# Up-projection by a Strassen-like scheme: weight sums made by adding DMAs, products accumulated in PSUM

## The chip, the cores and the metric

The kernel runs on one core of a Trainium2 chip. A core has a matrix engine (TensorE, PE in the profile; its weight loads are PEld), a vector engine (VectorE, DVE), a scalar engine (ScalarE, ACT), a general engine (GpSimd, POOL) and a sync engine (SP) that here only issues transfers (DMAs). Engines run side by side, each through its own instructions in order, and wait for each other through semaphores. SBUF is the working memory of 128 partitions; PSUM takes the products of TensorE in eight banks of 128x512 float32. The metric is device time in microseconds (us), the median of several runs.

## The reference

One layer of a decoder on 1024 tokens of width 1024: a mixer (pooling, a recurrence and a gate) with its output projection, then a squared-ReLU MLP, then a gated embedding, then a final norm. What matters here is the MLP:

```python
z = rms_norm(h, norm_mlp_g[l])                                    # [1024, 1024]
h = h + jnp.square(jax.nn.relu(z @ w_up[l])) @ w_down[l]          # w_up [1024, 4096]
```

Everything is float32.

## The kernel before

**Tiles and products.** Each float32 operand is split into a high part, rounded to the format that TensorE multiplies, and a low remainder. A product is hi·hi + hi·lo + lo·hi, three matmuls. `split` (L181) makes the parts: ScalarE copies the high part (L184), VectorE subtracts it (L185).

**The up-projection** (`up_first`, `up_pair`; tiles `ps_P_u`) computes 256 of the 4096 columns at a time, a pair of 128-column blocks, so 16 pairs (`NPAIR`). A pair is a 2x2 block product with both the 1024 rows of the weight and the 1024 tokens cut in two. A scheme of the Strassen-Winograd kind makes it with seven block products P1 to P7 instead of eight. Each product has four row tiles times three matmuls of 128x128 by 128x512, that is 12 matmuls (`product`, L815, through `mm`, L357). Four of the seven need sums of weight blocks, and the four results are sums of products. Sums of activation blocks are made once, at the end of the output projection (L790 to L796), and stay in the `a` and `y` tiles as split operands: P6, P7, P4 and P5 read `a`, and P1, P2 and P3 read `y`.

**Weights.** `up_step` brings them in four steps a pair. `load_up` (L240) loads the pair's blocks A11, A12, A21 and A22 with two 512 KB DMAs on SP's queue. VectorE makes the sums in place (`dv`, L226, rows of L227), and two products at a time are split into a high and a low tile (`split_weights`). For the first pair GpSimd makes three of the sums (`gp`, L229) in the tile `rstd` (called `R` in the code) and in the raw tile. There are two high and two low weight tiles of two products each. The list `todo` holds all weight steps of the kernel in order, and `weights()` (L353) starts the next step before it hands out the oldest, so weights are one step ahead of the product that uses them.

**Results.** Each product has a PSUM bank of its own. ScalarE copies some out (`copy`, L864) and VectorE adds the others to them (`add_got` and `add_both`, through `add`, L823). `finish_up` (L842) multiplies by the norm and clips at zero (L845, VectorE), squares (L847, ScalarE), makes four sums for the down-projection (L227) and stores seven blocks by four DMAs (L858, L859). It runs for a pair after the second product of the next one. The result tiles `cc` alternate between two pairs.

**Around it.** Before it stands the output projection (`ps_o`), whose last matmul ends at 225.5 us. In it the second norm collects its squares (`norm.add`, L408) in `T[4]`, with `T[5]` as its scratch; the norm itself is used in pair 1 (four matmuls `n_ps`, L438 and L439). Behind it stands the down-projection (`ps_P_d`), whose operands take the place of the `y` tiles (`open_down`) and of one half of the `a` tiles (`prepare`), as the last pair leaves them.

**Order.** The order on each engine is made ahead of time by a planner that follows the order of the program as its priority and issues an instruction once, by its own estimates, what it needs is ready. On the chip each engine then keeps that order.

Of the kernel before, what the change touches and what calls it, by code (L numbers as in the profile page):

```python
# [13 lines left out]
P = 128  # L14
# [48 lines left out]
def block_kernel(  # L63
# [152 lines left out]
    def split_weights(name, *srcs):  # L216

        hi, lo = weight_tiles(name)
        n = 0
        for src in srcs:  # L220
            w = src.shape[-1]
            split(src, hi[:, n : n + w], lo[:, n : n + w])
            n += w
        return [(hi[:, hs], lo[:, hs]) for hs in HALVES]

# [3 lines left out]
    def gp(op, to, x, y):  # L229
        return nc.gpsimd.tensor_tensor(to, x, y, op).ins  # L230

    up_raw, up_spare, up_lower, up_fourth = {}, [], {}, []

    def load_up(m):  # L240
        if m >= NPAIR:
            return
        up_raw[m] = [raw_tile(f"wu{m}_{i}") for i in range(2)] if m % 2 == 0 else up_spare
        for i, hs in enumerate((slice(0, S), slice(S, 2 * S))):
            nc.sync.dma_start(up_raw[m][i], w_up[m][:, hs])

    def up_blocks(m):
        a, b = up_raw[m]
        return a, b, a[:, FIRST], a[:, SECOND], b[:, FIRST], b[:, SECOND]

    def up_step(m, step):
        name = f"wu{m}_{step}"
        if m == 0:
            if step == 0:
                load_up(0)
            a, b, a11, a12, a21, a22 = up_blocks(0)
            s1, s2 = (R[:, hs] for hs in HALVES)
            if step == 0:
                gp(ALU.add, s1, a21, a22)
                gp(ALU.subtract, s2, s1, a11)  # L260
                gp(ALU.subtract, a21, a11, a21)
                return split_weights(name, s2, a21)
            if step == 1:
                w = split_weights(name, a22, s1)
                load_up(1)
                return w
            if step == 2:
                w = split_weights(name, a11, a12)
                up_lower[0, 3] = lowest[0]
                dv(ALU.subtract, a12, a12, s2)  # L270
                return w
            return split_weights(name, a12)
        a, b, a11, a12, a21, a22 = up_blocks(m)
        s1 = T[5][:, HALVES[m % 2]]
        if step == 0:
            w = split_weights(name, a)
            with tc.issue_after(up_lower[m - 1, 3]):
                dv(ALU.add, s1, a21, a22)
            with tc.issue_after(lowest[0]):
                dv(ALU.subtract, a11, s1, a11)  # L280
                up_fourth[:] = [dv(ALU.subtract, a12, a12, a11)]
            return w
        if step == 1:
            w = split_weights(name, a)

            dv(ALU.subtract, a21, a22, a11)
            load_up(m + 1)
            return w
        w = split_weights(name, b if step == 2 else s1)
        up_lower[m, step] = lowest[0]  # L290
        return w

# [48 lines left out]
    todo += [(up_step, m, step) for m in range(NPAIR) for step in range(4)]  # L341
# [424 lines left out]
    for o in range(NT):  # L766
        nc.sync.dma_start(H[o], xT[o * P : (o + 1) * P, :])
        if o == 0:

            out_w = {0: weights(), 1: asked.pop(0)}  # L770
            for i in range(2):
                out_ps[i] = psum(f"ps_o{i}")
                out_parts(i, out_w[i], out_ps[i], range(NT - 2))
        elif o == 1:
            ask()
        else:
            out_w[o], out_ps[o] = weights(), psum(f"ps_o{o}")
# [12 lines left out]
        if o % 2 == 1:  # L790
            z11, z12, z21, z22 = (T[i][:, hs] for i in range(2) for hs in HALVES)
            t2, t3, t4, t1 = (T[i][:, hs] for i in (2, 3) for hs in HALVES)
            for to, x, y in ((t1, z12, z11), (t2, z22, t1), (t3, z22, z12), (t4, z21, t2)):
                nc.vector.tensor_tensor(to, x, y, ALU.subtract)
            split(T[2], *A[o // 2])
            split(T[3], *A[4 + o // 2])  # L796
# [37 lines left out]
    def twice(x):  # L834
        return x.unsqueeze(1).broadcast_to([P, 2, x.shape[-1]])

    def up_sums(m):
        cc = t_all[:, 2 * (m % 2) : 2 * (m % 2) + 2]
        c11, c12, c21, c22 = (cc[:, i, hs] for i in range(2) for hs in HALVES)
        return cc, c11, c12, c21, c22, T[4 if m else 5][:, HALVES[m % 2]]  # L840
# [40 lines left out]
    done = []  # L881

    def up_first():
        cc, c11, c12, c21, c22, s = up_sums(0)
        ps = {}
        ws = {}
        for kinds in (("P6", "P7"), ("P4", "P5")):
            for kind, w in zip(kinds, weights()):
                ws[kind] = w
                ps[kind] = mlp_bank(f"ps_{kind}_u0")  # L890
                product(ps[kind], w, lambda t, kind=kind: up_operand(kind, t), range(3))
        for kind in ("P6", "P7", "P4", "P5"):
            product(ps[kind], ws[kind], lambda t, kind=kind: up_operand(kind, t), range(3, 4))
        with tc.issue_after(up_lower[0, 3]):
            up_second(NT - 1)
            norm.add(H[NT - 1])
            copy(s, ps["P5"])
            norm.casts()
        ws["P1"], ws["P2"] = weights()
        ws["P3"], _ = weights()  # L900
        for kind in ("P1", "P2"):
            ps[kind] = mlp_bank(f"ps_{kind}_u0")
            product(ps[kind], ws[kind], lambda t, kind=kind: up_operand(kind, t))
        product(ps["P5"], ws["P3"], lambda t: up_operand("P3", t), more=True)
        copy(c11, ps["P1"])
        add_got(c12, ps["P6"], c11)
        add_got(c22, ps["P7"], c12)
        add_got(c11, ps["P2"])
        add_got(c21, ps["P4"], c22)
        add(c22, s)  # L910
        add_got(c12, ps["P5"])
        done.append((0, cc))

    def up_pair(m):
        cc, c11, c12, c21, c22, s = up_sums(m)

        def of(kind, w):
            ps = mlp_bank(f"ps_{kind}_u{m}")
            product(ps, w, lambda t: up_operand(kind, t))
            return ps  # L920

        wa, wb = weights()
        if m == NPAIR - 1:
            preload_down()
        copy(s, of("P1", wa))
        add_got(c11, of("P2", wb), s)
        if m > 1:
            store_up = finish_up(*done.pop())
            if m < NPAIR - 1:
                store_up()  # L930
        else:
            norm.rstd(R, norm.sums(cast=True))
            leave("hl")
        wa, wb = weights()
        copy(c12, of("P3", wb))
        add_got(s, of("P6", wa))
        wa, wb = weights()
        if m == NPAIR - 1:
            with tc.issue_after(open_down()):
                store_up()  # L940
        add_got(c22, of("P7", wa), s)
        if m == NPAIR - 1:
            ask()
            prepare(0, 0)
        add_got(c21, of("P4", wb), c22)
        if m == 1:
            with tc.issue_after(up_lower[1, 2]):
                finish_up(*done.pop())()
        wa, _ = weights()
        p5 = of("P5", wa)  # L950
        if m == NPAIR - 1:
            for tp in range(1, NQ):
                prepare(0, tp)

        with tc.issue_after(up_fourth[0]) if m < NPAIR - 1 else ExitStack():
            add_both(cc[:, :, SECOND], p5)
        add(c12, s)
        done.append((m, cc))


# [6 lines left out]
    def open_down():  # L967
# [9 lines left out]
        for q in range(2, NQ):  # L977
            load_w(0, 0, q)
# [30 lines left out]
    def down(n):  # L1009
# [3 lines left out]
        def operand(t):  # L1013
            return half(A[4 * (n % 2) + t // 2], t % 2)

        for q in range(NQ):
# [13 lines left out]
            if n == q == 0:  # L1030
# [4 lines left out]
                finish_up(*done.pop())()  # L1035
# [54 lines left out]
    for m in range(1, NPAIR):  # L1090
        up_pair(m)
    norm2 = Norm("n2", T[0], T[1:2])
# [382 lines left out]
```

## Time and profile before

| | before |
|---|---|
| median of three runs | 919.4 us (919.05 to 919.93) |
| span of the profiled execution | 917.9 us |
| that execution's own time | not listed apart; the runs lie 1.5 us above its span |
| TensorE busy | 910.4 us, 99% of the span, 4227 matmuls |
| VectorE busy | 762.9 us, 83% |
| ScalarE busy | 443.5 us, 48% |
| GpSimd busy | 27.0 us, 3% |
| DMA, hardware queue | 128.38 MB, 42.0% of 16 engines |
| up-projection | 225.49 to 516.46 us |

A row of a group names the line, the engine, the operation, output and input tiles by the program's names, their shapes and the count; then the busy time, the mean in ns of one, and the idle time of the engine just before them with what ended it. A row of the chain has a start, a length and what filled it. L367 is the helper that issues nearly all matmuls; the tile tells the stage. `SPq` is SP's DMA queue.

### The profile page before, as it was taken

To read this page: it belongs to the slowest core of one execution; us is meant where nothing else is said; L and a number is where in the kernel's file an instruction comes from. 1 tells how busy PE (TensorE), PEld (TensorE's weight loads), DVE (VectorE), ACT (ScalarE), POOL (GpSimd) and SP (SyncE) were. 2 spreads that over 40 slices of the span, in tenths; PEclk is the share of its full clock that TensorE was granted. 3 is DMA by queue.
4 is the path that set the end of the run, shared out by engine and by line. 5 is a ranking of instruction groups with operands and counts; after the bars stand their busy time and mean duration, and the time that the engine had idled before them with its cause. 6 is when DMAs were issued, how large, how long until landed. Compare 5 with 4: busy or idle time off the path is not lost.

```text
span 917.9 us, 10985 instructions
## 1 busy us (share of the span) xinstructions
PE 910.4 (99%) x4227; PEld 792.5 (86%) x4227; DVE 762.9 (83%) x892; ACT 443.5 (48%) x517; POOL 27.0 (3%) x38
## 2 busy tenths in 40 slices
PE   9999999999999999999999999999999999999997
PEld 7888888888888888888888888888888888888886
DVE  7898984669998888888888989899877579799676
ACT  6568992447543343334333654344343346656223
POOL 3400000002000000000000000000000000000001
PEclk9999999999999999999999999999999999999999
DMA  8311143211255345435543998466633341032353
GB/s 270 101 51 32 38 169 107 69 46 62 77 164 192 127 154 195 156 126 172 198 135 135 320 370 279 132 197 208 200 112 125 114 161 47 1 115 70 93 183 126
DMA packets 49636, 129.07 MB, mean 141 GB/s; under 512 B 4400, under 2 KB 9392, under 8 KB 49584
## 3 DMA queue, kind: packets, MB, share of 16 engines
q1 hardware_dynamic: 49584, 128.38, 42.0%
q8 instruction: 33, 0.54, 0.2%
q14 instruction: 19, 0.16, 0.1%
HBM read 92.71 MB, written 35.65 MB: 140 GB/s over the span
## 4 chain that ended last, share of the span: by engine, by line
PE 98%; issue 1%; DVE 0%; DVEq 0%; ACT 0%; POOLq 0%; POOL 0%
PE ps_P_u L367 32%; PE ps_P_d L367 32%; PE ps_i L367 9%; PE ps_o L367 9%; PE ps_e L367 8%; PE ps_l L367 3%; PE ps_e L1223 2%; PE ps_l L574 1%; PE ps_j L367 1%; PE ps_g L643 1%; PE ps_p L367 1%; PE ps_l_second L367 1%; PE ps_l L524 0%; PE ps_j L1247 0%; PE ps_e L1247 0%
## 5 line engine op out<-in xcount | busy, mean ns | idle before, releaser
L367 PE MATMUL ps_P_d<-a,wd_P_hi 128*128 128x512 f32 x880 | 261.7, 379 | 0.0
L367 PEld LDWEIGHTS ps_P_d<-a,wd_P_hi 128*128 128x128 f32 x880 | 166.3, 189 | 23.6
L367 PE MATMUL ps_P_d<-a,wd_P_lo 128*128 128x512 f32 x440 | 166.8, 379 | 0.0
L367 PE MATMUL ps_P_u<-a,wu_hi 128*128 128x512 f32 x512 | 152.3, 379 | 0.0
L367 PE MATMUL ps_P_u<-y,wu_hi 128*128 128x512 f32 x384 | 114.2, 379 | 0.0
L367 PEld LDWEIGHTS ps_P_u<-a,wu_hi 128*128 128x128 f32 x512 | 96.8, 189 | 13.8
L367 PE MATMUL ps_P_u<-a,wu_lo 128*128 128x512 f32 x256 | 97.0, 379 | 0.0
L367 PEld LDWEIGHTS ps_P_d<-a,wd_P_lo 128*128 128x128 f32 x440 | 83.2, 189 | 12.0
L367 PEld LDWEIGHTS ps_P_u<-y,wu_hi 128*128 128x128 f32 x384 | 72.6, 189 | 10.2
L823 DVE TENSOR_TENSOR t_h<-t_h,ps_P_u 128x512 f32<-128x512 f32 (+1 forms) x80 | 62.5, 781 | 20.2 <-PE ps_P_u L367 20.2
L367 PE MATMUL ps_P_u<-y,wu_lo 128*128 128x512 f32 x192 | 72.8, 379 | 0.0
L823 DVE TENSOR_TENSOR t_h<-t_h,ps_P_d 128x512 f32<-128x512 f32 (+1 forms) x56 | 42.5, 759 | 33.5 <-PE ps_P_d L367 33.5
L185 DVE TENSOR_TENSOR a<-wd,a 128x1024 fp32r<-128x1024 f32 x56 | 67.2, 1219 | 1.1 <-ACT a L184 0.8
L367 PE MATMUL ps_i<-a,wi_hi 128*128 128x512 f32 x256 | 66.1, 381 | 0.0
L367 PE MATMUL ps_o<-y,wo_hi 128*128 128x512 f32 x256 | 65.7, 379 | 0.0
L184 ACT ACTIVATE a<-wd 128x1024 fp32r<-128x1024 f32 x56 | 58.2, 1051 | 14.3 <-PE ps_P_d L367 7.0
L184 ACT ACTIVATE wu_hi<-wu 128x1024 fp32r<-128x1024 f32 x24 | 25.4, 1057 | 69.7 <-PE ps_P_u L367 48.4
L184 ACT ACTIVATE wu_hi<-wu_raw 128x1024 fp32r<-128x1024 f32 (+1 forms) x26 | 25.2, 975 | 66.6 <-PE ps_P_u L367 39.5
L367 PEld LDWEIGHTS ps_i<-a,wi_hi 128*128 128x128 f32 x256 | 48.1, 189 | 8.0 <-issue 0.7
L367 PEld LDWEIGHTS ps_o<-y,wo_hi 128*128 128x128 f32 x256 | 48.4, 189 | 6.9
L367 PEld LDWEIGHTS ps_P_u<-a,wu_lo 128*128 128x128 f32 x256 | 48.4, 189 | 6.8
L184 ACT ACTIVATE wd_P_hi<-wd 128x1024 fp32r<-128x1024 f32 x24 | 25.3, 1055 | 53.2 <-PE ps_P_d L367 51.4
(258 smaller groups left out, 1497.1 us busy)
## 6 DMA issues: line engine op xcount, KB each, us to landing
wd<-act SPq DMA_DIRECT2D x56, 512.0 KB, 5.4
act<-t_h SPq DMA_DIRECT2D x32, 512.0 KB, 4.7
wu_raw<-in_w_up SPq DMA_DIRECT2D x16, 512.0 KB, 3.9
wu<-in_w_up SPq DMA_DIRECT2D x16, 512.0 KB, 4.0
act<-wu SPq DMA_DIRECT2D x16, 512.0 KB, 5.0
wd<-in_w_down SPq DMA_DIRECT2D x16, 512.0 KB, 5.6
t_h<-in_xT SPq DMA_DIRECT2D x14, 512.0 KB, 4.6
wg_raw<-in_w_gate SPq DMA_DIRECT2D x10, 512.0 KB, 3.3
```

The lines of the kernel that those rows point to most:

```text
L184: first = pin(nc.scalar.activation(hi, src, AF.Copy))
L185: lowest[:] = [pin((eng or nc.vector).tensor_tensor(lo, src, f32(hi), ALU.subtract)).ins]
L367: ins = nc.tensor.matmul(ps, w, turns(z[:, hs]), start=first and z is zhi and w is whi, stop=last and w is wlo, skip_group_check=more,)
L574: nc.tensor.matmul(ps, kblk(w, o), turns(z[:, hs]), start=k == n == 0, stop=False)
L643: nc.tensor.matmul(x, w[r, o * P : (o + 1) * P], turns(z[r, at : at + HALF]), start=n == 0, stop=n == 2)
L823: (eng or nc.vector).tensor_tensor(to, to if y is None else y, x, ALU.add)
L1223: nc.tensor.matmul(pg, z, turns(quad[x == 1][:, k]), start=n == 0, stop=n == 3 * NT - 1, skip_group_check=True)
```

## The change

Only the up-projection and its edges change. The seven products remain, 12 matmuls each.

- The signs of the scheme change so that the weight of P3 is the sum of all four blocks, P6's is A21 + A22 + A11, P5's A21 + A22 and P7's A21 + A11 (P1 takes A11, P2 A12, P4 A22).
- The weight sums are made by DMAs that add to what lies in their destination (`grow`, issued by GpSimd). A tile is loaded with A21 twice, one adding DMA of both halves makes P5's and P7's weights, and once P5's is split a second one makes P6's, then a third P3's in the same place. Each adding DMA waits until both parts of the split before it are made. Pair 0's tile is made in `R` during the output projection (`seed_up`). The last pair's P3 has a tile of its own.
- The weights are split product by product (`up_weight`), into one tile that holds the high and the low half; there are four of these tiles. `up_first` begins with one more `ask()`, so weights are two products ahead. A22 has a tile of its own (half of `T[5]`), and loads for a pair start up to two pairs ahead.
- In the middle pairs products are accumulated on each other in PSUM: ScalarE copies P1 out negated into the bank of P6, and P6, P7 and (in the next pair) P4 are accumulated onto it; P2 is accumulated onto P1's bank and P3 onto P5's. ScalarE copies the sums out in between; VectorE takes two differences a pair (`take`).
- The order of the products becomes P1, P5, P4 of the pair before, P6, P2, P3, P7. The last pair has an order of its own (`up_last`): P1, P5, P2, P3, P4 of the pair before, P4, P6, P7, and the down-projection's first operands take the other half of the `a` tiles.
- The host lays the weight out in the order A22, A11, A12, A21.

The core of the diff:

```diff
-    def split_weights(name, *srcs):
...
-    def gp(op, to, x, y):
-        return nc.gpsimd.tensor_tensor(to, x, y, op).ins
...
+    up_raw, up_lower, up_spare, up_place = {}, {}, [], itertools.cycle(("whi", "wlo"))
+    A22, A11, A12, A21 = (slice(n * HALF, (n + 1) * HALF) for n in range(4))
+
+    def twice(x):
+        return x.unsqueeze(1).broadcast_to([P, 2, x.shape[-1]])
+
+    def grow(to, src):
+        nc.gpsimd.dma_start(to, src, accum_op=ALU.add)
+
+    def seed_up():
+
+        halves = R.rearrange("p (y s) -> p y s", y=2)
+        nc.sync.dma_start(halves, twice(w_up[0][:, A21]))
+        for x in range(2):
+            grow(R[:, HALVES[x]], w_up[0][:, A22])
+        grow(R[:, SECOND], w_up[0][:, A11])
 
     def load_up(m):
...
+        a, c = [raw_tile(f"wu{m}_{i}") for i in range(2)] if m % 2 == 0 else up_spare
+        up_raw[m] = a, c, T[5][:, HALVES[m % 2]], c[:, FIRST] if m else R[:, SECOND]
+        w = w_up[m]
+        if m:
+            nc.sync.dma_start(c.rearrange("p (y s) -> p y s", y=2), twice(w[:, A21]))
+            grow(c, w[:, : 2 * HALF])
+        else:
+            nc.sync.dma_start(c[:, SECOND], w[:, A21])
+            grow(c[:, SECOND], w[:, A11])
+        nc.sync.dma_start(a, w[:, A11.start : A12.stop])
+        nc.sync.dma_start(up_raw[m][2], w[:, A22])
+        if m == NPAIR - 1:
+            nc.sync.dma_start(T[4][:, FIRST], w[:, A21])
+            for x in (A22, A11, A12):
+                grow(T[4][:, FIRST], w[:, x])
...
+    def up_weight(m, kind):
...
+        w = wp.tile([P, S], F32R, tag=next(up_place), name=f"wu{m}_{kind}")
+        hi, lo = (w[:, hs] for hs in HALVES)
+        split(src, hi, lo)
+        up_lower[m, kind] = lowest[0]
+        if kind == "P5" and not first:
+            grow(chain, w_up[m][:, A11])
+        elif kind == "P6" and not last:
+            grow(chain, w_up[m][:, A12])
+        elif kind == ("P4", "P3")[first] and m < NPAIR - 2:
+            load_up(m + 2)
+        elif first and kind == "P7":
+            load_up(1)
+        return hi, lo
...
             out_w = {0: weights(), 1: asked.pop(0)}
+            seed_up()
...
+    def up_open(m):
+
+        cc, c11, c12, c21, c22 = up_sums(m)
+        a, d = bank(f"ps_a_u{m}"), bank(f"ps_d_u{m}")
+        up_product(m, "P1", a)
+        if m < NPAIR - 1:
+            chains[m] = banks(f"ps_b_u{m}")[:, :HALF]
+            nc.scalar.activation(chains[m], a, AF.Copy, scale=-1.0)
+        else:
+            copy(c12, a)
+        up_product(m, "P5", d)
+        copy(c22, d)
+        return a, d
+
+    def up_fourth(m):
+        cc, c11, c12, c21, c22 = up_sums(m)
+        ps = chains.pop(m)
+        up_product(m, "P4", ps, more=True)
+        copy(c21, ps)
+        return finish_up(m, cc)
 
     def up_pair(m):
...
+        a, d = up_open(m)
+        b = chains[m]
         if m > 1:
+            up_fourth(m - 1)()
         else:
             norm.rstd(R, norm.sums(cast=True))
             leave("hl")
...
+        up_product(m, "P6", b, more=True)
+        copy(c12, b)
+        up_product(m, "P2", a, more=True)
+        copy(c11, a)
+        up_product(m, "P3", d, more=True)
+        take(c12, d, c12)
         if m == 1:
...
+            finish_up(0, up_sums(0)[0])()
+        up_product(m, "P7", b, more=True)
+        take(c22, b, c22)
...
-                split(X[tp], *A[4 * (n % 2) + tp])
+                split(X[tp], *A[4 * ((n + 1) % 2) + tp])
...
-    wu = np.asarray(w_up)[0].reshape(NT // 2, 2, P, NPAIR, 2, P).transpose(3, 2, 4, 1, 0, 5)
+    wu = np.asarray(w_up)[0].reshape(NT // 2, 2, P, NPAIR, 2, P).transpose(3, 4, 1, 2, 0, 5)
+    wu = np.stack([wu[:, i, j] for i, j in ((1, 1), (0, 0), (0, 1), (1, 0))], axis=2)
```

More of the change, by code (lines that the diff above doesn't have):

```diff
@@ L1 @@
+import itertools
 from contextlib import ExitStack
@@ L240, in load_up @@
-    def load_up(m):
[L241 to L291, printed above, removed]
@@ L905, in up_first @@
+        up_product(0, "P3", ps["P5"], more=True)
         copy(c11, ps["P1"])
-        add_got(c12, ps["P6"], c11)
-        add_got(c22, ps["P7"], c12)
+        take(c12, ps["P6"], c11)
+        add_got(c21, ps["P7"], c12)
         add_got(c11, ps["P2"])
[L909 to L912, printed above, removed]
-    def up_pair(m):
[L915 to L926, printed above, removed]
+        dv(ALU.subtract, c22, c21, c22)
@@ L976, in open_down @@
             last = load_x(0, tp)
-        for q in range(2, NQ):
-            load_w(0, 0, q)
+        load_w(0, 0, 2)
         for q in range(2):
@@ L1089, in block_kernel @@
     up_first()
-    for m in range(1, NPAIR):
+    for m in range(1, NPAIR - 1):
         up_pair(m)
+    up_last()
     norm2 = Norm("n2", T[0], T[1:2])
```

131 lines of the change are left out of this document (70 added, 61 removed).

## The prediction

> **What bounds the kernel now.** I read the page first, then the chain of waits in order of time, then the up stage by windows, then its instructions by shape. The first two fences are the page's head and rows of the chain (start in us, length in us, what).
>
> ```profile
> span 917.9 us, 10985 instructions
> PE 910.4 (99%) x4227; PEld 792.5 (86%) x4227; DVE 762.9 (83%) x892; ACT 443.5 (48%) x517; POOL 27.0 (3%) x38
> ```
>
> ```profile
> 225.49 23.34 PE ps_P_u L367 x108
> 248.83 0.22 PE n_ps L438
> ...
> 249.47 0.22 PE n_ps L439
> 249.69 266.77 PE ps_P_u L367 x1236
> 516.46 290.09 PE ps_P_d L367 x1344
> ...
> 899.79 5.19 PE ps_e L1223 x24
> 904.98 0.02 issue
> ```
>
> The up-projection runs from 225.49 to 516.46, 290.97 us, with 108 + 4 + 1236 = 1348 matmuls: 0.2158 us each. The down-projection next to it, which the change leaves its matmuls, needs 290.09 / 1344 = 0.2158. The pieces of the chain join end to end and all are TensorE's, so the stage holds no stall that a lighter VectorE could give back. The windows say the same (busy time and count per engine, granted clock, DMA share, GB/s).
>
> ```profile
> core 0: us, PE busy (x) PEld busy (x) DVE busy (x) ACT busy (x) POOL busy (x), PEclk, DMA share, GB/s
> 225.00:516.00 291.00, 291.00 (x1350) 254.63 (x1349) 259.07 (x305) 121.11 (x145) 0.00 (x0) 1.00 0.47 157
> 516.00:806.00 290.00, 290.00 (x1346) 253.80 (x1345) 238.76 (x240) 132.73 (x142) 0.00 (x0) 1.00 0.50 169
> ```
>
> VectorE is 89% busy in the stage (259.07 of 291) and TensorE 100% at a granted clock of 1.00. VectorE is nearly full, but it is nobody's wait.
>
> **The change part by part.** The matmuls first: seven products of 12 matmuls for each of 16 pairs, before and after; no size, clock or operand width changes. Cost 0. One product is 12 x 0.2158 = 2.59 us, a pair 18.13.
>
> VectorE and ScalarE, by shape inside the stage (count, busy us and mean ns of one, idle before):
>
> ```profile
> L823 DVE TENSOR_TENSOR t_h<-t_h,ps_P_u 128x512 f32<-128x512 f32 x65 | 44.3, 681 | 20.2 <-PE ps_P_u L367 20.2
> L845 DVE SCALAR_TENSOR_TENSOR t_h<-t_h,rstd 128x2048 f32<-128x2048 f32 x15 | 34.3, 2284 | 0.0
> L185 DVE TENSOR_TENSOR wu_lo<-wu,wu_hi 128x1024 fp32r<-128x1024 f32 x24 | 29.3, 1221 | 1.8 <-ACT wu_hi L184 1.3
> L184 ACT ACTIVATE wu_hi<-wu 128x1024 fp32r<-128x1024 f32 x24 | 25.4, 1057 | 69.7 <-PE ps_P_u L367 48.4 <-DVE wu L227 19.8 <-PE n_ps L439 1.5
> L864 ACT ACTIVATE t_h<-ps_P_u 128x512 f32<-128x512 f32 x32 | 18.7, 587 | 6.1 <-PE ps_P_u L367 5.9
> L823 DVE TENSOR_TENSOR t_h<-t_h,ps_P_u 128x1024 f32<-128x1024 f32 x14 | 17.0, 1214 | 0.0
> L227 DVE TENSOR_TENSOR wu<-t_h,wu 128x512 f32<-128x512 f32 x8 | 5.5, 691 | 0.2
> L185 DVE TENSOR_TENSOR wu_lo<-t_h,wu_hi 128x512 fp32r<-128x512 f32 x15 | 10.3, 684 | 0.0
> L184 ACT ACTIVATE wu_hi<-t_h 128x512 fp32r<-128x512 f32 x15 | 9.5, 630 | 12.8 <-PE ps_P_u L367 12.8
> ```
>
> Removed from VectorE: the four weight sums of pairs 1 to 15, 60 x 0.69 = 41 us, and most sums of products: 65 + 14 reads of PSUM fall to 5 (pair 0), 28 (two in each of pairs 1 to 14) and 3 (last pair, one of them wide), and 12 sums of two SBUF tiles go: 30 x 0.681 + 13 x 1.214 + 12 x 0.68 = 44 us less. Added: a pair's lower halves go from 3 x 1.221 + 0.684 = 4.35 to 7 x 0.684 = 4.79 us, 7 us in all. VectorE falls from 259 to about 180 us. ScalarE gets 76 copies of products for 32, 44 x 0.587 = 26 us, and 7 x 0.630 for 3 x 1.057 + 0.630 in upper halves, 9 us: 121 becomes about 156 us of 291. Both stay far from full and lie beside matmuls: worth 0, gain and loss. Were that cover gone, the 35 us on ScalarE would count in full.
>
> The new dependences on a copy have room. Starts within a middle pair: P1 0, P5 2.59, P4 of the pair before 5.18, P6 7.77, P2 10.36, P3 12.95, P7 15.54. ScalarE seeds P6's bank with -P1 from 2.59 on, 0.6 us for a bank wanted at 7.77; P2 goes onto P1's bank at 10.36; P3 onto P5's at 12.95, whose copy starts at 5.18; P7 onto P6's at 15.54, copied from 10.36. At least 4 us of slack each: 0. Queued behind such a copy on ScalarE is the next upper half, wanted two products later. For the stores, rows of VectorE and of SP's queue in one pair (start, length):
>
> ```profile
> 303.45 2.29 DVE L845 SCALAR_TENSOR_TENSOR t_h<-t_h,rstd 128x2048 f32<-128x2048 f32 x1
> ```
>
> ```profile
> 303.59 0.33 SPq L245 DMA_DIRECT2D wu_raw<-in_w_up  x1
> ...
> 310.88 0.45 SPq L859 DMA_DIRECT2D act<-wu  x1
> ```
>
> The results of a pair are finished one product later than before (after P4 in place of P2), so their stores start 2.6 us later; the buffer is rewritten 18.13 + 5.18 - 8.5 = 14.8 us after the finishing starts, against 310.88 + 5.2 (landing of a 256 KB store, below) - 303.45 = 12.6 now: 0, with some 2 us to spare.
>
> What is new on the path that could set the end are the **adding DMAs**. In pair m one 128x512 tile holds P5's weight (A21 + A22), then by an adding DMA P6's (+ A11), then by another P3's (+ A12). Each waits until both halves of the split before it have read the tile, and the next split waits for it. There are four weight slots of one product each, so product j can be split once product j-3 starts; for P5 that is P3 of the pair before. The loop from P3 to P3 is therefore: split P5 (0.630 + 0.684), a DMA, split P6 (0.630 + 0.684), a DMA, upper half of P3 (0.630) = 3.26 + 2L, L being the time from one adding DMA's release to its landing. If VectorE is in the middle of L845 when P5's lower half is due, it is 5.54 + 2L. It has 18.13 us: TensorE stalls only from **L = 6.3** (5.54) or **7.4** (3.26) on, and each us above costs 2 us in each of 14 pairs.
>
> L itself no trace shows. The nearest rows (KB each, median us from issue to landing; then POOL by time, start and length):
>
> ```profile
> wu<-in_w_up SPq DMA_DIRECT2D x16, 512.0 KB, 4.0
> act<-wu SPq DMA_DIRECT2D x16, 256.0 KB, 5.2
> out<-late SPq DMA_DIRECT2D x2, 256.0 KB, 2.1
> t_h<-in_xT SPq DMA_DIRECT2D x3, 256.0 KB, 5.7
> ```
>
> ```profile
> 213.04 2.14 POOL L230 TENSOR_TENSOR rstd<-rstd,wu_raw 128x512 f32<-128x512 f32 x1
> 215.13 1.29 POOL L230 TENSOR_TENSOR wu_raw<-wu_raw,wu_raw 128x512 f32<-128x512 f32 x1
> ```
>
> Lower bound: a quiet 256 KB copy, 2.1, with an issue like SP's, 0.33 (the first SP row above): 2.4. Upper bound: read the tile, then write it, each like the slowest 256 KB row, 2 x 5.7, with an issue as long as POOL's longest, 2.14: 13.5, which would be 3.26 + 27.0 - 18.13 = 12 us a pair, 170 in all. I take 4.0 + 1.3 = **5.3**: the 512 KB weight load, since it has the same source, stage and direction and twice the bytes (an add touches its tile twice), and POOL's short instruction for the issue. That is 1.0 under the lower threshold, so 0.
>
> By the Trainium skill (DMA: Bandwidth & Descriptors, Anatomy of one DMA), a POOL-issued DMA takes about 2.0 us plus bytes / 436e3, an estimate of 2.6 us for 256 KB; by it the margin would be 3.7 us and the sum the same. No run here shows it.
>
> The tightest place is **pair 1**: six products and the four norm matmuls (0.86). From P2 of pair 0 (238.4), which frees P5's slot, to P3 of pair 1 (254.8) are 16.4 us; with two VectorE instructions queued ahead (1.4), 4.6 + 2L gives a threshold of 5.9. Forecast 5.3: 0, by 1.2 us.
>
> Other moves. Loads: a pair issues three on SP (512, 512, 256 KB) for two, and three on POOL (512, 256, 256): 2.25 MB for 1.0, in 18.13 us 69 GB/s more, 226 for 157 GB/s, share 0.68 for 0.47, and about 0.85 if the tile read back counts too. Busy, not full. POOL's queue was empty in the stage; a large add for the pair after next can stand in it ahead of the second small one, but its plain load can start 10 us earlier, when P7's split has freed the tile. Pair 0's sums (four DMAs) start in the output projection, where POOL's three instructions end at 216.4; SP waits there for the norm tile with nothing urgent behind. Pair 0's A22 waits for the norm's last sum that reads its tile, and is wanted at 229.4, by the third product:
>
> ```profile
> 218.68 1.23 DVE L408 TENSOR_TENSOR t_h<-t_h 128x1024 f32<-128x1024 f32 x1 [0.20 <-ACT t_h L407]
> ```
>
> A load of 4.0 from 219.9 and a split of 1.3 end at 225.2. The last pair's P3 weight is three adds in a row, about 20 us, begun more than a pair ahead. At the hand-over to the down-projection four products stand between the last use of the y tiles and the first down product, as now, and two after the A tiles are free, as now. All 0.
>
> **Sum:** the profiled execution's span 917.9 + 0 = 917.9; the runs are 1.5 us above the span (919.4), so **919.4**.
>
> **The rivals.** (1) *The adding chain is too long*, slower. For it: L is unseen, it stands twice in a loop, DMA engines are busier. Against: every 256 KB row lies below 6.3. It decides from L = 6.3 to 7.4. At 8.0: 3.26 + 16.0 - 18.13 = 1.13 us a pair, x 14 = 16, so 935; if an add costs two passes of 4.0, L = 9.3, 3.73 x 14 = 52, so 971.
> (2) *VectorE holds up POOL's issue.* If each add also waited out one VectorE instruction (1.2 us, L185's wide form, before the change), L = 6.5, and with L845 ahead 5.54 + 13.0 - 18.13 = 0.41 a pair, 6 in all: 925. For it: VectorE stays 60% busy; against: POOL's row of 1.29 us at 215 stands beside a busy VectorE. The Trainium skill (SBUF — State Buffer, Who interferes with whom) has this starvation for VectorE copies and one-input forms on two ports, not for sums of two tensors, and the stage's rows are nearly all sums: by that rule it would not happen here.
> (3) *Only the start stalls*: pair 1, or the hand-over into it, at L between 5.9 and 8: 4.6 + 16 - 16.4 = 4.2 at most, about 923.
> (4) *The hand-over to the down-projection stalls* on SP's fuller queue: one 512 KB landing late, 4.0: 923.
> (5) *Faster*: only outside the stage, since TensorE has no gap inside: 1.5 us off the 12.9 us after TensorE's last chained matmul (904.98 to 917.9), 917.9.
> (6) *It doesn't do what it says*: the planner sets an order in which a product waits on its copy or its DMA for nothing; that looks like (1) or (3), and is in their chances.
>
> **How the numbers follow.** Forecast 0.55; (1) 0.20, of which half is above 945; (2) 0.07; (3) 0.10; (4) 0.05; (5) 0.03. Faster 0.03, same 0.55, slower 0.42, where 0.2% (1.8 us) is what a measurement of this kernel can tell. Forecast's own range 918.4 to 920.8. For 8 in 10 it must take in (2), (3), (4) and the lower half of (1), L up to about 8.4: 918.0 to 945. The bound L = 13.5 (1090) stays outside, with the upper half of (1).
>
> **What would show it.** Right: the up stage again 291 us of matmuls end to end; VectorE near 180 and ScalarE near 156 us in it; adding DMAs landing in under 6.3 us after the split that frees them. Wrong: TensorE idle before P6 or P3 with the releaser a DMA or a weight's upper half (1, 2); idle only between 243 and 256 (3); idle after 516 (4). The prediction fails if L is above 6.3 us or POOL's order holds a small add behind a large one.

## The result: 1017.3 us, 10.6% slower

The changed kernel takes 1017.33 us (median of 4 runs, 1015.16 to 1018.9) against 919.64 us (4 runs, 919.05 to 919.93) for the kernel before it: a ratio of 1.106, 95% interval 1.1045 to 1.1076. The prediction, 919.4 us in a range of 918 to 945, is wrong. The page's head and its chain by engine (share of the span) of the changed kernel:

```profile
span 1014.9 us, 11314 instructions
PE 939.7 (93%) x4227; PEld 802.5 (79%) x4227; DVE 681.8 (67%) x819; ACT 464.8 (46%) x606; POOL 68.8 (7%) x87
PE 63%; DMA 21%; DVE 7%; issue 5%; ACT 3%; POOL 1%; SPq 0%; DVEq 0%; POOLq 0%; ACTq 0%
```

The chain was all TensorE's; now a fifth of it is DMA. The span grew by 97.0 us, and the windows say where (stretch and its length, then busy time and count of each engine, granted clock, DMA share, GB/s):

```profile
225.00:614.00 389.00, 323.31 (x1363) 267.47 (x1362) 180.60 (x231) 143.86 (x235) 40.07 (x46) 0.93 0.64 173
614.00:905.00 291.00, 290.79 (x1347) 254.59 (x1348) 240.67 (x245) 132.87 (x144) 0.00 (x0) 1.00 0.50 164
```

The up-projection takes 389 us for the 291 before; the down-projection behind it still takes 291. The waits (in all, times, longest) are TensorE's first, then those of the splits and of GpSimd:

```profile
PE ps_b_u L358 <- ACT ps_b_u L911: 54.4, 13, 7.4
PE ps_d_u L358 <- ACT wu_P L185: 6.3, 5, 1.8
PE ps_d_u L358 <- ACT t_h L852: 2.8, 1, 2.8
PE ps_P_d L358 <- DVE a L186: 2.2, 1, 2.2
PE ps_e L1262 <- DVE ps_e L1247: 1.8, 2, 1.0
...
ACT wu_P L185 <- DMA wu_raw<-in_w_up: 116.3, 14, 13.2
ACT wu_P L185 <- DMA wu<-in_w_up: 88.2, 13, 9.5
POOL wu L227 <- DVE wu_P L186: 115.7, 15, 13.3
POOL wu_raw L227 <- DVE wu_P L186: 90.0, 11, 10.9
```

TensorE waits 67.5 us in these five rows, and its matmuls take 939.7 - 910.4 = 29.3 us longer: together 96.8 of the 97.0. The first row names a copy (L911, the seed of P6's bank), yet the copy isn't late by itself. One pair in order of time, on ScalarE, VectorE, GpSimd, SP and TensorE (start, length, instruction, idle before it and what ended that), shows what it stands behind:

```profile
402.42 0.63 ACT L185 ACTIVATE wu_P<-wu 128x512 fp32r<-128x512 f32 x1 [4.91 <-DMA wu<-in_w_up]
...
406.01 2.00 ACT L835 ACTIVATE t_h<-t_h 128x1024 f32<-128x1024 f32 x2 [1.47 <-DVE t_h L833]
...
422.67 0.63 ACT L185 ACTIVATE wu_P<-wu_raw 128x512 fp32r<-128x512 f32 x1 [12.61 <-DMA wu_raw<-in_w_up]
423.20 0.58 ACT L911 ACTIVATE ps_b_u<-ps_a_u 128x512 f32<-128x512 f32 x1
...
429.45 0.63 ACT L185 ACTIVATE wu_P<-wu_raw 128x512 fp32r<-128x512 f32 x1 [4.64 <-DMA wu_raw<-in_w_up]
```

```profile
403.69 2.29 DVE L833 SCALAR_TENSOR_TENSOR t_h<-t_h,rstd 128x2048 f32<-128x2048 f32 x1
405.89 0.69 DVE L186 TENSOR_TENSOR wu_P<-wu,wu_P 128x512 fp32r<-128x512 f32 x1
...
409.86 0.68 DVE L186 TENSOR_TENSOR wu_P<-wu_raw,wu_P 128x512 fp32r<-128x512 f32 x1
...
424.36 0.69 DVE L186 TENSOR_TENSOR wu_P<-wu_raw,wu_P 128x512 fp32r<-128x512 f32 x1 [0.34 <-ACT wu_P L185]
```

```profile
412.13 0.88 POOL L227 DMA_DIRECT2D wu<-in_w_up  x1 [14.19 <-DVE wu L218]
412.69 1.23 POOL L227 DMA_DIRECT2D wu_raw<-in_w_up  x1
424.37 0.86 POOL L227 DMA_DIRECT2D wu_raw<-in_w_up  x1 [10.46 <-DVE wu_P L186]
```

```profile
406.61 0.38 SPq L243 DMA_DIRECT2D wu<-in_w_up  x1
407.10 1.99 SPq L846 DMA_DIRECT2D act<-t_h  x2
```

```profile
414.25 2.75 PE L358 MATMUL ps_b_u<-a,wu_P 128*128 128x512 f32 x12
423.83 4.91 PE L358 MATMUL ps_b_u<-a,wu_P 128*128 128x512 f32 x12 [6.83 <-ACT ps_b_u L911]
```

Follow the weight tile. At 402.42 the second small addition (A12) of a pair has landed and P3's upper half starts. The next pair's P5 must be split before its first small addition (A11) may write, and its lower half ends at 410.54 (409.86 + 0.68): 8.12 us of work in a fixed order, in which P7's lower half and ScalarE's squares (L835) wait for VectorE's multiplication L833, and the upper halves of P1 and P5 for the squares. A11's transfer isn't issued at 410.54 but at 412.69, because the large addition stands ahead of it in GpSimd's queue and waits for its own plain load, which SP issued at 406.61, when P7's lower half had freed the tile. (The load landed at 411.51, 0.62 us before the large addition was issued. The bracket at 412.13 names a sum on VectorE, the last event that the profile saw; in run 5 it names another instruction, and the issue comes 0.62 us after the load's landing again.) A11 has landed by 422.67, when P6's upper half starts; P6's split lets A12 go at 424.37, and it has landed by 429.45. From 402.42 to 429.45 are 27.0 us, where TensorE has 18.13 us of work; at 423.83 it has been idle for 6.83 us.

Cut at these four points, a pair of any run is a sum of four terms. The table gives their means, in us, over the eleven loops that end in pairs 4 to 14 of each profile, from the starts and ends of the splits (L185 and L186 here): P3's upper half to the end of P5's lower half ("ordered"), from there to P6's upper half ("A11", with whatever holds its issue), P6's split, and from there to P3's upper half ("A12").

| run | ordered | A11 | P6's split | A12 | sum | median time |
|---|---|---|---|---|---|---|
| changed kernel | 8.12 | 10.05 | 1.35 | 5.67 | 25.2 | 1017.3 |
| 3, large on VectorE | 8.13 | 7.61 | 1.35 | 5.02 | 22.1 | 975.9 |
| 4, no accumulation | 8.13 | 8.71 | 1.35 | 4.20 | 22.4 | 979.5 |
| 5, squares late | 4.36 | 11.98 | 1.35 | 5.72 | 23.4 | 996.9 |
| 6, squares late, large behind | 5.41 | 4.87 | 1.35 | 6.91 | 18.5 | 932.2 |
| 7, squares late, large on VectorE | 8.11 | 4.71 | 1.35 | 7.03 | 21.2 | 967.6 |
| 9, large behind | 8.12 | 7.29 | 1.35 | 5.96 | 22.7 | 988.3 |
| 10, squares late, no large | 4.84 | 4.91 | 1.36 | 7.08 | 18.2 | 927.5 |

For the changed kernel 25.2 - 18.13 = 7.07 us a pair. There are thirteen such loops, into pairs 2 to 14; over all of them the mean is 25.02, so they make 13 x 6.89 = 90 us, and TensorE's waits at pair 1, at the hand-over to the down-projection and in the output stage add 2.8 + 2.2 + 1.8: 96.4 of the 97.0. Where a sum is near 18.13, TensorE sets it and the terms hold waits for a free weight slot as well.

The pair shown is of the slower of two kinds. In the next one the plain load is issued when P2's lower half is done (424.36 + 0.69), not P7's, and the large addition goes ahead of A11 by 7 us. GpSimd and SP there:

```profile
431.14 0.86 POOL L227 DMA_DIRECT2D wu_raw<-in_w_up  x1 [5.91 <-DVE wu_P L186]
437.93 0.86 POOL L227 DMA_DIRECT2D wu<-in_w_up  x1 [5.93 <-DVE wu_P L186]
```

```profile
425.08 0.38 SPq L243 DMA_DIRECT2D wu_raw<-in_w_up  x1
```

A11 (437.93) goes 0.36 us after P5's lower half ends, and nothing holds it. The two kinds alternate: in pairs 4, 6 to 14 A11's term is 11.85 us in the mean and the sum 26.8, in pairs 5, 7 to 13 they are 7.90 and 23.2.

### The profile page after: what moved, and what is told of

Read it like the earlier page. It is cut to its first block, busy times and chain, and to the rows that moved or that the text cites. A ratio compares the mean times of both kernels' runs of the same rounds, so it can differ in the third digit from the quotient of the medians.

```text
span 1014.9 us, 11314 instructions
## 1 busy us (share of the span) xinstructions
PE 939.7 (93%) x4227; PEld 802.5 (79%) x4227; DVE 681.8 (67%) x819; ACT 464.8 (46%) x606; POOL 68.8 (7%) x87
## 3 DMA queue, kind: packets, MB, share of 16 engines
q0 software_dynamic: 7488, 17.57, 10.6%
## 4 chain that ended last, share of the span: by engine, by line
PE 63%; DMA 21%; DVE 7%; issue 5%; ACT 3%; POOL 1%; SPq 0%; DVEq 0%; POOLq 0%; ACTq 0%
PE ps_P_d L358 28%; DMA wu<-in_w_up 10%; DMA wu_raw<-in_w_up 9%; PE ps_i L358 8%; PE ps_o L358 8%; PE ps_e L358 7%; DVE t_h L833 3%; PE ps_l L358 3%; DVE wu_P L186 2%; ACT wu_P L185 1%; PE ps_b_u L358 1%; ACT t_h L835 1%; PE ps_a_u L358 1%; PE ps_P_u L358 1%; PE ps_l L565 1%
## 5 line engine op out<-in xcount | busy, mean ns | idle before, releaser
L358 PE MATMUL ps_b_u<-a,wu_P 128*128 128x512 f32 x504 | 135.7, 424 | 54.4 <-ACT ps_b_u L911 54.4
L358 PEld LDWEIGHTS ps_b_u<-a,wu_P 128*128 128x128 f32 x504 | 105.1, 213 | 79.2 <-ACT ps_b_u L911 59.7
L186 DVE TENSOR_TENSOR wu_P<-wu_raw,wu_P 128x512 fp32r<-128x512 f32 x45 | 30.9, 688 | 103.3 <-ACT wu_P L185 103.3
L186 DVE TENSOR_TENSOR wu_P<-wu,wu_P 128x512 fp32r<-128x512 f32 x47 | 32.3, 687 | 80.2 <-ACT wu_P L185 80.2
L358 PE MATMUL ps_a_u<-y,wu_P 128*128 128x512 f32 x360 | 84.8, 384 | 0.0
L185 ACT ACTIVATE wu_P<-wu_raw 128x512 fp32r<-128x512 f32 x45 | 27.9, 621 | 116.6 <-DMA wu_raw<-in_w_up 116.3
L358 PEld LDWEIGHTS ps_a_u<-y,wu_P 128*128 128x128 f32 x360 | 68.3, 192 | 12.4 <-DVE wu_P L186 2.5
L185 ACT ACTIVATE wu_P<-wu 128x512 fp32r<-128x512 f32 x47 | 29.0, 621 | 93.5 <-DMA wu<-in_w_up 88.2
L186 DVE TENSOR_TENSOR a<-wd,a 128x1024 fp32r<-128x1024 f32 x56 | 67.2, 1219 | 1.8 <-ACT a L185 1.5
L185 ACT ACTIVATE a<-wd 128x1024 fp32r<-128x1024 f32 x56 | 58.1, 1049 | 13.1 <-PE ps_P_d L358 7.0
L358 PE MATMUL ps_d_u<-y,wu_P 128*128 128x512 f32 x180 | 45.2, 397 | 9.2 <-ACT wu_P L185 6.3
L185 ACT ACTIVATE wd_P_hi<-wd 128x1024 fp32r<-128x1024 f32 x24 | 25.3, 1054 | 52.6 <-PE ps_P_d L358 52.5
L358 PEld LDWEIGHTS ps_d_u<-y,wu_P 128*128 128x128 f32 x180 | 34.1, 195 | 18.9 <-ACT wu_P L185 8.3
```

Source lines behind the costliest of these rows:

```text
L185: first = pin(nc.scalar.activation(hi, src, AF.Copy))
L186: lowest[:] = [pin((eng or nc.vector).tensor_tensor(lo, src, f32(hi), ALU.subtract)).ins]
L358: ins = nc.tensor.matmul(ps, w, turns(z[:, hs]), start=first and z is zhi and w is whi, stop=last and w is wlo, skip_group_check=more,)
```

## The experiments

Times are compared with the runs of the kernel before on the same chip: 919.68 us for runs 1 to 4, 919.16 for 5 to 8, 919.46 for 9 to 12.

**Run 1: all sums of pairs 1 to 15 on VectorE.** The accumulation in PSUM, ScalarE's copies and the split product by product stay. In the last pair P7's A11 is added from a tile that has been refilled by then.

```diff
-            grow(c, w[:, : 2 * HALF])
...
+        if not first and kind in ("P5", "P7"):
+            dv(ALU.add, src, src, a22 if kind == "P5" else a[:, FIRST])
...
-            grow(chain, w_up[m][:, A11])
+            dv(ALU.add, chain, chain, a[:, FIRST])
...
-            grow(chain, w_up[m][:, A12])
+            dv(ALU.add, chain, chain, a[:, SECOND])
```

> The sums of the weights of pairs 1 to 15 are added by VectorE from tiles that are in SBUF already; the accumulation of products in PSUM, ScalarE's copies and the weights' split product by product stay. If the adding transfers are the cause, the up-projection's stage goes back to TensorE's own 291 us and the time to 918 to 925 us. If the accumulation in PSUM and ScalarE's copies and their order hold TensorE up (the trace shows TensorE waiting for a ScalarE copy), most of the 98 us stays: 980 to 1020.

Measured: 923.83 us (923.15 to 924.65), ratio 1.0044 (1.0027 to 1.006). The adding transfers are the cause; the copies and the accumulation cost the stage nothing. TensorE's waits in this run:

```profile
PE ps_P_d L361 <- DVE a L186: 2.3, 1, 2.3
PE ps_e L1265 <- DVE ps_e L1250: 1.8, 2, 1.0
PE ps_l L518 <- PEq L1480: 0.8, 1, 0.8
```

None is in the up-projection. The third was there before the change; the first two, at the hand-over to the down-projection and in the output stage, make the 4 us that remain. Both also stand in the changed kernel's waits above.

**Run 2: only the two small additions on VectorE.**

```diff
-            grow(chain, w_up[m][:, A11])
+            dv(ALU.add, chain, chain, a[:, FIRST])
...
-            grow(chain, w_up[m][:, A12])
+            dv(ALU.add, chain, chain, a[:, SECOND])
```

> Only the two small additions of each pair (A11 and A12, 256 KB each, the ones that stand in a chain with VectorE's and ScalarE's split) go to VectorE; the large one of 512 KB stays a transfer. If the loop of small transfer, split, small transfer, split is the cause, the time is 918 to 930. If the large transfer and GpSimd's queue behind it are, two thirds of the loss or more stay: 985 or above.

Measured: 924.51 us (923.62 to 925.39), within a microsecond of run 1. The window of the up-projection:

```profile
225.00:516.00 291.00, 291.00 (x1350) 254.83 (x1349) 194.19 (x254) 145.43 (x232) 14.73 (x17) 1.00 0.71 200
```

TensorE is busy without a gap while GpSimd still issues every large addition (512 KB, medians of 6.7 and 8.4 us to landing). An adding transfer outside the loop costs nothing; the loop, with what holds up its transfers, is the whole loss but for the 4 us of run 1.

**Run 3: only the large addition on VectorE**, with the first half of run 1's diff (and its last pair).

> Only the large addition (512 KB) goes to VectorE; the two small ones stay transfers in their chain. If the loop of the small ones is the cause by itself, at 8.2 us of ordered work, 1.7 of splits and two transfers of 5.0 to 5.5 us a pair takes some 20.0 to 21.0 us against TensorE's 18.1, so 28 to 43 us of the loss over 15 pairs stay: 948 to 963. If the large transfer's place in the queue is the whole cause: 918 to 930. If it has no part in it: 1010 to 1020.

Measured: 975.89 us (974.65 to 977.12). It lies above the interval that I gave to the loop by itself. The order is the 8.1 us I had read off the trace, but A11 takes 7.61 and not 5.0 to 5.5. It is issued at 416.13, amid four stores of results that SP issues from 412.33 to 417, and has landed 8.8 us later; in the next pair, again amid four stores, 6.4 us.

**Run 4: the same transfers without accumulation.**

```diff
-        nc.gpsimd.dma_start(to, src, accum_op=ALU.add)
+        nc.gpsimd.dma_start(to, src)
```

> All of GpSimd's transfers copy and don't add (the sums of the weights are left out, so the products are of other weights); their number, bytes, places in the queue and waits stay. If reading, adding and writing is what makes them slow, each falls well under 5 us and the time to 918 to 945. If it is the issue, the descriptors and the way from memory, the times per transfer stay within 0.5 us and the time at 1005 to 1020.

Measured: 979.48 us (977.33 to 981.62), between the two expectations. The issues of the changed kernel and then of this run (KB each, median us to landing):

```profile
wu<-in_w_up POOLq DMA_DIRECT2D x15, 256.0 KB, 6.6
rstd<-in_w_up POOLq DMA_DIRECT2D x4, 256.0 KB, 5.3
```

```profile
wu<-in_w_up POOLq DMA_DIRECT2D x15, 256.0 KB, 5.7
rstd<-in_w_up POOLq DMA_DIRECT2D x4, 256.0 KB, 3.9
```

Adding costs 0.9 to 1.4 us a transfer in these rows (1.5 in a third one, `wu_raw`, 5.6 against 4.1); in the table A11 loses 1.34 and A12 1.47, 2.8 a pair, 36 us over thirteen pairs for the 37.8 measured. Accumulation is less than half of the loss. Plain copies in this loop still cost 60 us.

**Run 5: the order changed.** L833 and the squares of a pair are issued behind the next pair's P5 split.

```diff
-            up_fourth(m - 1)()
+            up_fourth(m - 1)
...
         take(c22, b, c22)
+        finish_up(m - 1, up_sums(m - 1)[0], up_lower[m + 1, "P5"])()
...
+        with tc.issue_after(behind) if behind else ExitStack():
+            nc.vector.scalar_tensor_tensor(cc, cc, 0.0, twice(R), ALU.max, ALU.mult)
```

> All additions stay transfers, as in the changed kernel. Only the order on VectorE and ScalarE changes: the multiplication with ReLU (2.3 us) and the squares (2.0 us) of a pair stand behind the P5 split of the next pair, not ahead of it. If the loop of transfers and ordered work sets the period by itself, the ordered part falls from 8.2 to some 4.5 us and 40 to 60 us of the loss go: 955 to 980. If GpSimd's queue decides, because the large addition that stands ahead of the first small one waits for its own plain load, the small one starts no earlier and less than 20 us go: 997 to 1017.

Measured: 996.93 us (995.03 to 998.83), 20 us less, at the border of the second expectation. The order did fall as meant, 8.12 to 4.36, but A11 grew from 10.05 to 11.98. VectorE ends P5's lower half at 400.69; GpSimd and SP at that time:

```profile
403.81 0.88 POOL L227 DMA_DIRECT2D wu<-in_w_up  x1 [11.70 <-DVE t_h L875]
404.36 1.23 POOL L227 DMA_DIRECT2D wu_raw<-in_w_up  x1
```

```profile
398.71 0.38 SPq L243 DMA_DIRECT2D wu<-in_w_up  x1
```

A11 is ready 3.7 us before it is issued: the large addition ahead of it waits for a plain load issued at 398.71. Half of what the order gave was lost again in A11: in the mean of pairs 4 to 14 its issue is held 2.6 us for 1.4 before, and the transfer takes 0.8 us longer.

**Run 6: the order of run 5, and the large addition behind A12.**

```diff
-            grow(c, w[:, : 2 * HALF])
...
-            grow(chain, w_up[m][:, A12])
+            last_small = grow(chain, w_up[m][:, A12])
+            if not first:
+                with tc.issue_after(last_small.ins):
+                    grow_large(m + 1)
```

> The order of the run before this one, and the large addition for the next pair is issued behind the second small one of this pair, where its plain load has long landed, so that nothing holds GpSimd's queue ahead of the first small one. If the loop and the queue together are the cause, the period is 4.5 us of order, 1.7 of splits, two small transfers of 5 to 6.5 us and up to 2 us that the large one costs the next P5: 17 to 20 us, 920 to 950. If the time is in the transfers' own number and bytes, it stays with the run before this one or above.

Measured: 932.18 us (931.68 to 932.68), ratio 1.0141 (1.0121 to 1.0161). All additions are transfers as in the changed kernel, and 85 of its 98 us are gone. GpSimd's rows of a pair and a half:

```profile
397.06 0.86 POOL L227 DMA_DIRECT2D wu<-in_w_up  x1 [5.18 <-DVE wu_P L186]
397.74 1.07 POOL L227 DMA_DIRECT2D wu_raw<-in_w_up  x1
409.30 0.86 POOL L227 DMA_DIRECT2D wu_raw<-in_w_up  x1 [10.49 <-DVE wu_P L186]
415.74 0.89 POOL L227 DMA_DIRECT2D wu_raw<-in_w_up  x1 [5.57 <-DVE wu_P L186]
```

From A12 at 397.06 to A12 at 415.74 are 18.7 us. The large addition follows A12 at once, and A11 (409.30) goes when P5's lower half ends, with nothing ahead of it in the queue.

**Run 7: the order of run 5, the large addition on VectorE**, P7's part of it added right before P1's split so that the last pair is whole.

> The order of the two runs before this one, the large addition on VectorE, the two small ones as transfers. The loop is then 4.5 us of order, 1.7 of splits and two transfers of 4.5 to 7.5 us (8.9 and 6.4 for the first one, 4.4 for the second, in the run with the large addition on VectorE): 15 to 18.5 us against TensorE's 18.1. By the loop theory the loss is gone but for the 4 us at the hand-over and in the output: 921 to 930, with two transfers per pair in the chain. If any transfer in the chain costs by itself, 950 or more.

Measured: 967.62 us (966.8 to 968.43), far above 921 to 930. By its outcome it would speak for transfers that cost by themselves; its VectorE rows say otherwise:

```profile
434.36 0.69 DVE L218 TENSOR_TENSOR wu<-wu,wu 128x512 f32<-128x512 f32 x1 [4.09 <-DMA wu<-in_w_up]
434.96 0.68 DVE L186 TENSOR_TENSOR wu_P<-wu_raw,wu_P 128x512 fp32r<-128x512 f32 x1
```

The addition that I had moved to the front waits 4.09 us for its plain load, and P5's lower half waits behind it: the ordered term is 8.11 again, by a wait of my own making. The run tells nothing against the loop and didn't test it. Run 10 does.

**Run 8: run 1 with the last pair mended, and three entries in the list that the output stage counts.**

```diff
     up_last()
+    turn.extend(range(3))
```

> All sums of pairs 1 to 15 on VectorE, as in the first run, with the last pair's P7 added from its tile in time (the first and third run added it from a tile that was refilled already, which changes values and no time). Beside it three entries in the list by whose length the output stage chooses its PSUM tiles, so that it chooses as the kernel before does (143 entries there at the end of the up-projection, 38 after the change). If that choice is what puts TensorE's two waits of 0.79 and 0.96 us for VectorE's addition into the output stage, they go and the time is 1.5 to 2 us below the first run's 923.8: 921.8 to 922.3. If not, 923.5 to 924.

Measured: 922.60 us (921.1 to 924.28), ratio 1.0037 (1.0024 to 1.005), 0.3 us above what I gave. The profile settles it: its span is 920.0, 2.2 below run 1's, and the row for L1250 in TensorE's waits is gone. `ple_psum` takes its PSUM tiles by whether the length of `turn` is odd, and `mlp_bank` adds an entry per call, so asking for fewer banks in the up-projection changed the tiles of a stage 300 us later.

**Run 9: only the large addition behind A12**, run 6's diff with run 5's order taken back.

> All additions stay transfers and VectorE's and ScalarE's order is the changed kernel's; only the large addition for the next pair is issued behind the second small one of this pair. The loop theory adds 8.2 us of ordered work, 0.4 to the issue, 1.7 of splits and two small transfers of 4.4 to 5.5 us: 19.1 to 21.3 us a pair against 18.1, so 15 to 48 us of loss and 4 at the hand-over and in the output: 938 to 971. If GpSimd's queue alone were the cause: 925 to 933, as with the order changed too. If the order alone were: 1005 or above.

Measured: 988.32 us (988.19 to 988.46), above the loop's 938 to 971. The sum of the terms still holds, but A11 takes 7.29 us beside the stores of results, as in run 3, and A12 5.96 beside the large addition, where I had put 4.4 to 5.5 for each. So the order alone is worth 20 us (run 5), the queue alone 29, and both together 85. They don't add up, and the table says at which term: A11 stays at 12.0 with the order alone and at 7.3 with the queue alone, and falls to 4.9 with both. Without the queue's hold A11 goes when P5 is split, and the late squares bring most of the stores behind it (in run 6 the first two are issued at 412.32 and 413.99, A11 has landed at 413.92).

**Run 10: the order of run 5, the large addition left out.**

```diff
-            grow(c, w[:, : 2 * HALF])
```

> The large addition is left out (so the products P5, P7, P6 and P3 are of other sums), with its wait and its bytes; the two small ones stay in their chain, with the order of the fifth run and no add on VectorE that could wait for a load. The loop is 4.5 us of order, 1.7 of splits, two transfers of 4.4 to 6.5 us: 15 to 19.2 us. By the loop theory 921 to 935. If two adding transfers in the chain cost by themselves: 950 or more, as in the run with the large one on VectorE (967.6).

Measured: 927.54 us (927.34 to 927.73), ratio 1.0089. Two adding transfers a pair stand in the loop and the sum is 18.2, near TensorE's own 18.13. What is left lies elsewhere: waits of 3.1 us at pair 1, 1.4 at the hand-over and 1.7 in the output. Two transfers in a chain of splits don't cost by themselves.

**Run 11: run 8 with the first splits of the down-projection's operands ahead of pair 14's last sums.**

```diff
-                split(X[tp], *A[4 * ((n + 1) % 2) + tp])
+                with tc.high_priority(40) if n == 0 else ExitStack():
+                    split(X[tp], *A[4 * ((n + 1) % 2) + tp])
```

> The eighth run with the first splits of the down-projection's operands put ahead of the last sums of pair 14 on VectorE. TensorE's one wait left, 2.3 us at the hand-over to the down-projection, should go: 919.5 to 920.8, no difference from the kernel before. If the wait comes from the operands' loads, 922 to 923.

Measured: 921.81 us (921.05 to 922.54), ratio 1.0026 (1.0016 to 1.0037), worse than expected. TensorE's waits there:

```profile
PE ps_P_d L362 <- DVE wd_P_lo L186: 0.9, 1, 0.9
PE ps_P_d L362 <- DVE a L186: 0.2, 1, 0.2
```

The wait of 2.3 us shrank to 0.2, and 0.9 of it came back 13 us later at a weight's lower half: the splits I had put first moved the pair's multiplication with ReLU back on VectorE (527.52 for 525.19 in run 8), and the lower half stands behind the sums that follow it. Another 1.3 us of the 2.4 between this span (920.3) and the kernel before's (917.9) I can't name.

**Run 12: run 6 with both corrections.**

> The sixth run (all additions as transfers, squares late, large one behind) with the two corrections of the eighth and eleventh. Its profile showed TensorE waiting 1.1 us at the hand-over and 2.1 in the output: 928.5 to 929.5 if both go, 932 if they have no part.

Measured: 929.08 us (927.33 to 929.88), ratio 1.0103 (1.0088 to 1.0118), as expected: the wait in the output is gone, and the one at the hand-over fell from 1.1 to 0.5 us. No version here beats the kernel before.

## Why the prediction was wrong

**The step that failed** is the loop "from P3 to P3", 3.26 + 2L, which I put at 13.9 us. Of its 3.26, 1.94 was the way from P3's upper half to the end of P5's split: that upper half and one split, as if they followed each other. Measured it is 8.12. I had counted the instructions of the chain and not those that stand between them on two engines in program order: on ScalarE five instructions and the two squares, on VectorE L833, two more lower halves and two sums. I had allowed for L833 by itself (5.54 + 2L) but not for the squares behind it, which wait for it and which the splits wait for. With 8.12 the loop keeps up with TensorE only for L up to (18.13 - 8.12 - 1.31) / 2 = 4.35, less than the 5.3 that I took.

**The term L was too small** as well. Two of them were 10.6 and measured 15.72. A12 at 5.67 is near my 5.3, by luck, since I had put that together from a plain load and a sum on GpSimd. A11 at 10.05 holds the 4.9 of runs 6, 7 and 10, some 2.4 more beside the stores of results (7.29 in run 9, 7.90 in the odd pairs of the changed kernel), and in the even pairs (11.85) 4 more from the large addition ahead of it. Each error alone would have been mild: 8.12 + 1.35 + 10.6 is 20.1, 1.9 us a pair and 25 in all; 1.94 + 1.31 + 15.72 is 19.0, 11 in all. Together they are 7.1 a pair and 92.

**The queue.** I saw that "a large add for the pair after next can stand in it ahead of the second small one" and dismissed it, as "its plain load can start 10 us earlier". In every second pair it stands ahead of the first small one; there its load starts when P7's lower half is done, which L833 holds up, 5.5 us before the large addition is issued; and when that is issued it runs beside A11. Of the last sentence of my prediction both conditions came true.

**The rivals.** (1), the adding chain, was right in its direction and in its place; its price ended at 971 (1090 at the bound of L, outside my range) because I varied L alone. (3) is right in its place: TensorE waits 2.8 us at pair 1 in the changed kernel and 3.0 to 3.2 in runs 6, 10 and 12. (4) is right in its place, with 2.2 us of my 4.0, but it comes from VectorE's order (run 11), not from SP's queue. (2) didn't happen: with the queue free, A11 goes 0.4 us after P5's lower half (409.30 against 408.25 + 0.69 in run 6) while VectorE works on. That agrees with the rule of the Trainium skill that I named there (SBUF — State Buffer, Who interferes with whom).

**The dependences on copies** ("at least 4 us of slack each: 0") were right by run 1. In the changed kernel 54.4 us of wait carry the name of such a copy all the same. I had asked what is queued behind a copy; what mattered was what it is queued behind. It follows P6's upper half on ScalarE, which waits for A11.

**Right:** VectorE 180.6 us in the stage for about 180; ScalarE 143.9, 12 us less than my 156, which adds up durations, where instructions that follow each other overlap by 0.1 us (402.96 against 402.42 + 0.63 in the changed kernel); the seeds in the output projection; the stores, whose buffer nobody waits for; and the DMA share, 0.82 at 216 GB/s in run 6, where a pair takes nearly 18.13 us, for 0.68 to 0.85 and 226. The lighter VectorE brought nothing, since it had been nobody's wait. **Missed:** the output stage's PSUM tiles, 1.8 us, through a list that the diff doesn't show.

By the page that I cited for L, a transfer of 256 KB would take 2.6 us by estimate (the Trainium skill, DMA: Bandwidth & Descriptors, Anatomy of one DMA). The nearest that GpSimd issued here is 3.9, run 4's plain copies in a quiet stage, and an adding one took 5.3 there.

## What to carry to other kernels

A loop that goes through a DMA and back to an in-order engine is as long as everything that stands in program order between its links: walk each engine's queue from link to link, and add what each link waits behind, not only the links. A transfer that is needed soon should not be issued behind one that waits for a load of its own. When a wait names a short copy, look one instruction up its queue. And read two periods of a loop before you take one for all: here every second pair was of another kind.

## What the runs showed of the hardware that I had not expected

After a gap TensorE can run slow. After the gap of 6.83 us twelve matmuls took 4.91 us for 2.75, at a granted clock of 0.57 in that stretch, and shorter gaps do it too, though not always:

```profile
396.54 4.54 PE L358 MATMUL ps_b_u<-a,wu_P 128*128 128x512 f32 x12 [2.63 <-ACT ps_b_u L911]
...
446.29 2.86 PE L358 MATMUL ps_b_u<-a,wu_P 128*128 128x512 f32 x12 [2.00 <-ACT ps_b_u L911]
```

Nine such places, behind gaps of 2.63 to 7.37 us, make about 20 of the 29 us by which TensorE's matmuls take longer, with a granted clock of 0.93 over the stage. The other 9 lie at the full clock, in products of 2.86 to 3.15 us and at the ends of products before a gap, and I haven't followed them. None of it came on top of the loop: in pairs 4 to 14 the ordered term is 8.12 or 8.13 in each, and A11 and A12 end with their landings, so no term waits for TensorE, and faster matmuls would only have waited longer.

The Trainium skill (TensorE: Matmul & The Clock Gate, What's actually happening) has half the clock after an idle window of some 3.4 us; the gap of 6.83 agrees, the one of 2.63 is shorter and was followed by slow matmuls as well, and one of 3.12 (before 498.21) was not.

An adding transfer holds GpSimd longer than a plain one, 0.86 us (412.13 and 424.37 above: 0.88 and 0.86) for 0.54 in run 4, and takes 0.9 to 1.4 us more to land:

```profile
403.64 0.54 POOL L227 DMA_DIRECT2D wu_raw<-in_w_up  x1 [8.73 <-DVE wu_P L186]
```

Beside other transfers the same 256 KB took twice as long: from issue to landing A11 needed 4.6 us beside a plain load and, from 412.32 on, a store and a second load (409.30 to 413.92 in run 6), and 10.8 beside the large addition, a plain load and two stores (404.36 to 415.11 in run 5).
